# Inverses of the scan's 64x64 triangles from 8x8 blocks by products of I + powers, and decays in 65 columns a chunk

## The chip, the cores and the metric

The kernel runs on 1 core of one Trainium2 chip. The metric is the device time of one execution in microseconds (us); the time of a kernel is the median over its runs.

## The reference, cut to what matters

The program computes two blocks of a diffusion-like model and a mixture of experts. The change lies in the recurrence of the first block, which runs twice (once in each of its two layers), over a context of 256 tokens and then 512 tokens, in both directions, for 8 heads of 64 channels:

```python
def wkv_scan(r, k, v, decay, kk, a, s0, reverse, emit):
    xs = tuple(jnp.swapaxes(t, 0, 1) for t in (r, k, v, decay, kk, kk * a))

    def step(s, inp):
        r_t, k_t, v_t, w_t, kk_t, b_t = inp
        sa = -jnp.einsum("bhvk,bhk->bhv", s, kk_t)
        s = (s * w_t[:, :, None, :] + sa[..., None] * b_t[:, :, None, :]
             + v_t[..., None] * k_t[:, :, None, :])
        y = jnp.einsum("bhvk,bhk->bhv", s, r_t) if emit else None
        return s, y
...
        decay = jnp.exp(-DECAY_SCALE * jax.nn.sigmoid(decay_b0[d] + jnp.tanh(w_lo) @ decay_up[d]))
        a = jax.nn.sigmoid(iclr_b0[d] + a_lo @ iclr_up[d])
```

In chunks of 64 tokens the recurrence becomes matrix products. Inside a chunk the terms `sa` depend on one another through a strictly triangular 64x64 matrix N, so each chunk, head and direction needs the inverse (I - N)^-1.

## The kernel before, in words

All engines execute their own instruction stream in order; the tile framework orders the streams from the program's generators at build time. TensorE is PE here, VectorE DVE, ScalarE ACT, GpSimd POOL, SyncE SP.

**Steps of a scan.** `scan` runs 12 steps per layer: 4 pairs of heads, and for each pair 3 groups of 256 tokens (4 chunks). A step handles both directions and the two heads of the pair, which lie in partitions 0 to 63 and 64 to 127 and so in opposite quadrants of PE. `chunks` (L979 on) is the recurrence itself. For every chunk and direction it makes the right-hand side psR on PE (L986, L989), negates it on DVE (L992), multiplies by the inverse XI on PE (psS, L996), copies the result on ACT (L998), makes the new state psM on PE (L1004), scales the old state on POOL (L1008), adds the two on DVE (L1009), and makes the outputs pyo on PE (L1016, L1019).

**Work laid between.** `among` walks through the chunks and lets two other streams advance beside them: `others` (convolution, modulation weights, outputs of finished pairs) and `to_come`, which prepares the later steps. In step s it runs `inverse_of(s + 1)`, `blocks_of(s + 2)` and `decays(s + 3)`.

- `decay` (L849 to L876): two products pz on PE, tanh on ACT, a running sum over 64 columns a chunk on DVE (L863) with one subtraction forward (L866) or two operations backward (L870, L871), and three exponentials on ACT: P and Pp (decay up to and before a token) and Pi.
- `products` (L887 to L913): six multiplications of 128x256 on DVE, then the products pg on PE (L906), masked on DVE into GM (L910, L913). N is one half of a GM tile.
- `solve` (L680 to L694): writes N to DRAM (`nsc`, 2 DMAs for each direction, on SP), the backward direction after a 32x32 transpose on DVE (L680), reads back the 64 diagonal blocks of 16x16 as one tile NB of 64 partitions, inverts the blocks by 14 pairs of small DVE operations (L689, L690) and writes them to `xsc` in DRAM.
- `solved` (L702): loads the block inverses of a step with 4 DMAs. `transposed` copies transposes of keys and values by PE and ACT (pt L925, L926; pv L932, L933).
- `inverse` (L948 to L967): merges 16 to 32 and 32 to 64. For each level and direction: a transpose on DVE (L948), 8 products N X on PE (py, L954), a copy on ACT (L957), 8 products with XI on PE (pw, L963), and a predicated copy on DVE into the off-diagonal part (L967).

Before step 0 the streams run one after the other: `decays(0)`, `blocks_of(0)`, `decays(1)`, `inverse_of(0)`, `blocks_of(1)`, `decays(2)`.

In the trace one fp32 matmul leaves two MATMUL records; 16 products of 64x64 are 32 records. `scanbuf`, `XT` and `RK` are large buffers in which the scan's small tiles lie, so that rows name them and not N, X or XI.

Of the kernel before, what the change touches and what calls it, by code (L numbers as in the profile page):

```python
# [28 lines left out]
CH = 64  # L29
# [19 lines left out]
OTHERS = [14] * 12  # L49


def shape_constants():
# [16 lines left out]
    cf["scan"] = np.broadcast_to((np.arange(256) % CH != 0).astype(np.float32), (128, 256))  # L69
    ci = []  # L70
    for d in range(2):
        for m in (16, 32):
            pm, fm = p % 64 // m, f[:, 0:64] // m
            if d == 1:
                pm, fm = fm, pm
            ci.append(((pm // 2 == fm // 2) & (pm % 2 == 0) & (fm % 2 == 1)).astype(np.float32))
# [6 lines left out]
    return cat(cols[0]), names, cat(ci + cols[1])  # L83


NMASK = 4 * 64
# [42 lines left out]
def tile_two_blocks(ctx: ExitStack, tc: tile.TileContext, I: dict, out: bass.AP, dump=None, stop=None):  # L129
# [39 lines left out]
    CM = wk.tile([128, NMASK], I8, name="CM")  # L169
    CB = wk.tile([128, nm - NMASK], BF16, name="CB")  # L170
    cmf = wk.tile([128, nm], F32, name="cmf", tag="big", bufs=4)
    nc.gpsimd.dma_start(cmf, I["const_m"])
    nc.gpsimd.tensor_copy(CM, cmf[:, 0:NMASK])
    nc.gpsimd.tensor_copy(CB, cmf[:, NMASK:nm])
# [463 lines left out]
    def scan_buffers(first_time, RK):  # L638
# [4 lines left out]
        for name, n, cnt in (("GM", 1024, 6), ("KR", 512, 6), ("Z", 512, 4), ("BT", 512, 4), ("XI", 256, 4), ("BK", 512, 4), ("XY", 512, 2),  # L643
                             ("Mn", 128, 4)):
            ring[name] = []
            for _ in range(cnt):
                sp = next(q for q in spans if q[1] + n <= q[0].shape[1])
                ring[name].append(sp[0][:, sp[1]:sp[1] + n])
                sp[1] += n
        if first_time:  # L650
            z = SB[0][:, 0:64 * BP // 128]
# [16 lines left out]
    BP = 128 * 16 + 16  # L668
    NSC, XSC = ([dr.tile([1, 64 * BP], F32, name=f"{n}{i}") for i in range(2)] for n in ("nsc", "xsc"))
    blocks = lambda t: t[0].rearrange("(b x) -> b x", x=BP)[:, 0:2048].rearrange("b (i t) -> b i t", t=128)[:, :, 0:16]  # L670
# [3 lines left out]
    def solve(s, T, gs):  # L674

# [7 lines left out]
        NB = wk.tile([64, 16, 16], F32, name="NB", tag="nb", bufs=1)  # L683
        nc.sync.dma_start(NB, blocks(NSC[s % 2]))
        yield
        for k in range(1, 15):
            t = wk.tile([64, 64], F32, name="nbt", tag="nbt", bufs=1)[:, 0:k * (15 - k)].rearrange("p (a b) -> p a b", a=k)
            sh = [64, k, 15 - k]
            nc.vector.tensor_tensor(t, NB[:, 0:k, k:k + 1].to_broadcast(sh), NB[:, k:k + 1, k + 1:16].to_broadcast(sh), op=OP.mult)  # L689
            nc.vector.tensor_tensor(NB[:, 0:k, k + 1:16], NB[:, 0:k, k + 1:16], t, op=OP.add)  # L690
            if k % 2:
                yield
        nc.vector.tensor_scalar(NB.rearrange("p a b -> p (a b)")[:, 0:256:17], ones[0:64, 0:16], 1.0, None, op0=OP.mult)
# [3 lines left out]
    def solved(s, T, gs, get):  # L697
        for q, (d, _) in zip(T, gs):
            XI, XY = get("XI").rearrange("p (c t) -> p c t", c=4), get("XY").rearrange("p (a c t) -> p a c t", a=2, c=4)
            q.update(XI=XI, X=XY[:, 0], Y=XY[:, 1])  # L700
            for h in range(2):
                nc.sync.dma_start((q["X"] if d else q["XI"])[HR[h]], own(XSC[s % 2], d, h))  # L702

    def scan(l, S):
# [43 lines left out]
        def inverse_of(s):  # L748
            solved(s, Ts[s], parts(s)[2], get)
            yield from every(transposed, s)  # L750
            yield from inverse(Ts[s], parts(s)[2])
# [90 lines left out]
    def decay(q, l, S, pr, d, g):  # L842
# [9 lines left out]
        tA = wk.tile([128, 4, 256], F32, name="tA", tag="spl", bufs=4)  # L852
        tB = wk.tile([128, 4, 256], F32, name="tB", tag="spl", bufs=4)
        c4 = lambda v: v.rearrange("p (c t) -> p c t", t=CH)
        sa = tA[:, 0:2]
        for i in range(2):
            nc.scalar.activation(tA[:, i], pz[i][:, 0:256], AF.Tanh, scale=0.5,
                                 bias=HB[:, 8 * i + 4 * d + pr:8 * i + 4 * d + pr + 1])
        nc.scalar.activation(sa, sa, AF.Copy, scale=0.5, bias=0.5)
        yield  # L860
        sg, a = tA[:, 0], tA[:, 1]
        cum, oth = tA[:, 2], tA[:, 3]
        nc.vector.tensor_tensor_scan(cum, cst("scan"), sg, 0.0, op0=OP.mult, op1=OP.add)  # L863
        P, Pi, Pp, tmp = tB[:, 0], tB[:, 1], tB[:, 2], tB[:, 3]
        if d == 0:
            nc.vector.tensor_tensor(oth, cum, sg, op=OP.subtract)  # L866
            incl, excl = cum, oth
# [9 lines left out]
        q.update(ts=ts, a=a, P=P, Pi=Pi, Pp=Pp, tmp=tmp)  # L877
        yield

    def products(q, l, S, pr, d, g, KK, get, emit):  # L880

        RK = S["RK"]
        ts, a, P, Pi, Pp, tmp = (q[n] for n in ("ts", "a", "P", "Pi", "Pp", "tmp"))
# [3 lines left out]
        nc.vector.tensor_tensor(KR[:, 0], KK[:, ts], Pp, op=OP.mult)  # L887
        nc.vector.tensor_tensor(tmp, KK[:, ts], a, op=OP.mult)
        nc.vector.tensor_tensor(BK[:, :, 1], c4(tmp), c4(Pi), op=OP.mult)
        nc.scalar.activation(a, a, AF.Identity, scale=vc("k_a", 4 * l + pr), bias=KC[:, pr, 0:1])  # L890
        nc.vector.tensor_tensor(a, a, RK[:, 1, pr % 2, ts], op=OP.mult)
        nc.vector.tensor_tensor(BK[:, :, 0], c4(a), c4(Pi), op=OP.mult)
        if emit:
            nc.vector.tensor_tensor(KR[:, 1], RK[:, 0, pr % 2, ts], P, op=OP.mult)

        PC = wk.tile([128, 4], F32, name="PC", tag="pc", bufs=6)
        nc.vector.tensor_copy(PC, c4(P)[:, :, 63 if d == 0 else 0])
# [39 lines left out]
    def inverse(T, gs):  # L937

        bc = lambda v: v[:, None, :].to_broadcast([128, 4, 64])
        ch4 = lambda v: v[:, 0:256].rearrange("p (c t) -> p c t", c=4)  # L940

        def each(f):
            for q, (d, _) in zip(T, gs):
                f(q, d)

        def first(q, d):
            a = ("X", "XI") if d == 0 or i else ("XI", "X")
            nc.vector.transpose(q[a[0]], q[a[1]])  # L948

        def left(q, d):  # L950
            q["p"] = ch4(bank("iv", None, "py"))
            for c in range(4):
                for h in range(2):
                    nc.tensor.matmul(q["p"][HR[h], c], lhsT=q["NT"][HR[h], c], rhs=q["X"][HR[h], c], start=True, stop=True)  # L954

        def out_(q, d):
            nc.scalar.activation(q["Y"], q["p"], AF.Copy)  # L957

        def right(q, d):
            q["p"] = ch4(bank("iv", None, "pw"))  # L960
            for c in range(4):
                for h in range(2):
                    nc.tensor.matmul(q["p"][HR[h], c], lhsT=q["Y"][HR[h], c], rhs=q["XI"][HR[h], c], start=True, stop=True)  # L963

        def merge(q, d):
            mk = CM[:, (2 * d + i) * 64:(2 * d + i + 1) * 64]
            nc.vector.copy_predicated(q["XI"], bc(mk), q["p"])  # L967

        for i in range(2):
            for f in (first, left, out_, right, merge):  # L970
                each(f)
                yield
# [1209 lines left out]
```

## Time and profile before

| | |
|---|---|
| median of 3 runs | 4025.75 us (4024.86 to 4033.54) |
| the profiled execution | 4035.13 us, its span 4033.3 us |
| busy over the span | PE 3787.4 (94%), PEld 2847.6 (71%), DVE 2757.5 (68%), ACT 1707.5 (42%), POOL 330.9 (8%) |
| window taken for the first scan, from its first psS | 347 to 690 us |
| window taken for the second scan | 1581 to 1891 us |

Busy is the union of an engine's records in time. A matmul record of 64 columns lasts 0.22 us, but the next one starts long before it ends, so that PE is shown busy through the tail of each short burst. What PE could still take has to be read from how closely records follow each other. PEld is the loading of weights, which overlaps the matmuls. A row of the groups view gives the count, the busy time, the mean length of one, and the idle time of the engine just before with what ended it. The four sections of the page that this document uses are the busy times, the groups, the windows and the timeline.

### The profile page before, as it was taken

The page shows a single profiled execution, that of the slowest core. Times are in us where ns is not written, and L with a number is a line of the kernel's source. Part 1 is how long each engine was busy: PE and PEld are TensorE (multiplying, and loading weights), DVE is VectorE, ACT ScalarE, POOL GpSimd, SP SyncE. Part 2 cuts the span into 40 slices and gives each one's busy share as a digit, 9 for nine tenths or more (in the row PEclk, how much of TensorE's full clock was granted, in tenths as well). Part 3 has the DMA queues.
Part 4 walks back from the last instruction along what each step waited for, and adds up shares of the span by engine and source line. Part 5 has one row for each costly group of instructions (what it writes and reads, how often), then busy time and mean ns, then how long its engine had stood idle before and what let it go on. Part 6 is the DMA issues. An engine that isn't in the chain of part 4 may idle for free. (4 is left out here: it accounts for less than half of the span.)

```text
span 4033.3 us, 69782 instructions
## 1 busy us (share of the span) xinstructions
PE 3787.4 (94%) x27963; PEld 2847.6 (71%) x27963; DVE 2757.5 (68%) x5535; ACT 1707.5 (42%) x2552; POOL 330.9 (8%) x301
## 2 busy tenths in 40 slices
PE   6998999999999998899999998997999999999997
PEld 4786777788888786776787786675565777764443
DVE  4778875753433778876745455657877899987776
ACT  3234352321212334442322244544655676666565
POOL 0000111000000000110000000001101122122111
PEclk8999999999999998899999998997999999999999
DMA  6122323332422221123545421035979899998996
GB/s 206 44 79 67 113 65 95 124 126 84 126 79 90 96 71 27 32 42 107 164 138 165 108 81 42 1 117 186 348 289 347 304 360 369 369 353 327 373 370 241
DMA packets 353980, 677.87 MB, mean 168 GB/s; under 512 B 118760, under 2 KB 230195, under 8 KB 323539
## 3 DMA queue, kind: packets, MB, share of 16 engines
q1 hardware_dynamic: 343024, 636.89, 45.1%
q0 software_dynamic: 9376, 34.63, 3.4%
q8 instruction: 221, 3.62, 0.4%
q10 hardware_dynamic: 1250, 1.85, 0.1%
q14 instruction: 109, 0.89, 0.1%
HBM read 635.39 MB, written 37.90 MB: 167 GB/s over the span
## 5 line engine op out<-in xcount | busy, mean ns | idle before, releaser
L431 ACT ACTIVATE wh<-wst 128x1024 fp32r<-128x1024 f32 (+2 forms) x222 | 222.8, 1004 | 988.9 <-PE pc L441 519.9
L1795 DVE TENSOR_TENSOR ml<-E,mh 128x2048 fp32r<-128x2048 f32 x236 | 536.1, 2286 | 92.0 <-PE pu L1843 44.3
L1794 ACT ACTIVATE mh<-E 128x2048 fp32r<-128x2048 f32 x236 | 447.7, 1916 | 187.6 <-PE pu L1843 147.5
L441 PE MATMUL px<-Hh,wl 128*128 128x512 f32 (+2 forms) x1216 | 485.9, 400 | 15.6 <-DVE wl L432 15.5
L441 PE MATMUL px<-Hh,wh 128*128 128x512 f32 (+3 forms) x1216 | 485.3, 401 | 13.6 <-ACT wh L431 7.1
L441 PE MATMUL px<-Hl,wh 128*128 128x512 f32 (+3 forms) x1216 | 484.7, 399 | 1.0 <-DVE Hl L419 1.0
L432 DVE TENSOR_TENSOR wl<-wst,wh 128x1024 fp32r<-128x1024 f32 (+2 forms) x222 | 255.4, 1152 | 270.5 <-ACT wh L431 268.2
L1843 PE MATMUL pu<-ml,ch 128*64 128x512 f32 (+2 forms) x968 | 273.0, 399 | 21.1 <-DVE ml L1795 20.9
L1843 PE MATMUL pu<-mh,ch 128*128 128x512 f32 (+1 forms) x968 | 280.2, 404 | 6.9 <-DVE ch L1831 4.2
L441 PEld LDWEIGHTS px<-Hh,wl 128*128 128x128 f32 (+1 forms) x1216 | 231.0, 190 | 74.7 <-DVE wl L432 20.9
L441 PEld LDWEIGHTS px<-Hh,wh 128*128 128x128 f32 (+1 forms) x1216 | 231.4, 191 | 72.9 <-ACT wh L431 9.7
L441 PEld LDWEIGHTS px<-Hl,wh 128*128 128x128 f32 (+1 forms) x1216 | 231.2, 190 | 57.0 <-DVE Hl L419 5.0
L533 DVE SCALAR_TENSOR_TENSOR acc<-ZC,VT,acc 128x272 f32<-128x272 f32 (+2 forms) x600 | 253.6, 479 | 2.6 <-ACT acc L528 2.5
L1843 PEld LDWEIGHTS pu<-mh,ch 128*128 128x128 f32 (+1 forms) x968 | 172.4, 185 | 86.8 <-issue 25.4
L1795 DVE TENSOR_TENSOR ml<-st,mh 128x2048 fp32r<-128x2048 f32 x86 | 196.0, 2286 | 42.8 <-PE pu L1843 24.5
L1843 PEld LDWEIGHTS pu<-ml,ch 128*64 128x64 f32 (+2 forms) x968 | 149.8, 159 | 90.7 <-DVE ml L1795 32.3
L441 PE MATMUL pc<-Hh,wh 128*128 128x256 f32 x672 | 192.9, 288 | 0.9 <-ACT Hh L418 0.9
L441 PE MATMUL pc<-Hl,wh 128*128 128x256 f32 x672 | 191.7, 285 | 0.5 <-DVE Hl L419 0.5
L441 PE MATMUL pc<-Hh,wl 128*128 128x256 f32 (+1 forms) x672 | 190.4, 284 | 0.1
L1794 ACT ACTIVATE mh<-st 128x2048 fp32r<-128x2048 f32 x86 | 163.2, 1917 | 55.4 <-PE pu L1843 31.7
L315 DVE SCALAR_TENSOR_TENSOR as<-adt,CS,as 128x512 f32<-128x512 f32 x224 | 161.3, 747 | 33.8 <-DMA adt<-in_w_ada_dram 19.4
L1099 DVE SCALAR_TENSOR_TENSOR XT<-px,MOD,XT 128x512 f32<-128x512 f32 x66 | 49.5, 750 | 188.9 <-PE px L441 188.6
(596 smaller groups left out, 7949.8 us busy)
## 6 DMA issues: line engine op xcount, KB each, us to landing
E<-in_w_mlp_dram SPq DMA_DIRECT2D x288, 1024.0 KB
st<-in_w_mlp_dram SPq DMA_DIRECT2D x94, 1024.0 KB
wst<-in_w_in_dram SPq DMA_DIRECT2D x29, 1024.0 KB
adt<-in_ada_w_dram SPq DMA_DIRECT2D x96, 256.0 KB
adt<-in_w_ada_dram SPq DMA_DIRECT2D x96, 256.0 KB
wst<-in_ffn_wg_dram SPq DMA_DIRECT2D x22, 1024.0 KB
wst<-in_ffn_wu_dram SPq DMA_DIRECT2D x22, 1024.0 KB
adaw<-in_ada_w_dram SPq DMA_DIRECT2D x16, 1024.0 KB
```

The costliest lines, as they stand in the source:

```text
L315: nc.vector.scalar_tensor_tensor(acc[s], t, c, acc[s], op0=OP.mult, op1=OP.add)
L431: nc.scalar.activation(wh, t[:, :, c0:c0 + n], AF.Copy)
L432: nc.vector.tensor_tensor(wl, t[:, :, c0:c0 + n], f32(wh), op=OP.subtract)
L441: nc.tensor.matmul(p[0:m, 0:n], lhsT=wa[:, k, 0:m], rhs=ha[:, k, a:a + n], start=k == 0 and first, stop=k == nk - 1 and last)
L533: nc.vector.scalar_tensor_tensor(o, z[:, j + a:j + a + n], cw(j), o, op0=OP.mult, op1=OP.add)
L1099: nc.vector.scalar_tensor_tensor(o, src, gate, o, op0=OP.mult, op1=OP.add)
L1794: nc.scalar.activation(wh, t, AF.Copy)
L1795: nc.vector.tensor_tensor(wl, t, f32(wh), op=OP.subtract)
L1843: nc.tensor.matmul(p[0:xa.shape[2]], lhsT=xa[:, kt], rhs=w[part][:, c:c + 512], start=kt == 0 and j == 0, stop=last and j == len(parts) - 1)
```

## The change

The constant masks for the merges are gone; a mask `scoff` (1 outside the 8x8 diagonal blocks) comes in.

- **`solve`**: blocks of 8x8 instead of 16x16, so NB has 128 partitions and 6 pairs of DVE operations of 6 to 12 columns. After the DMAs to `nsc` are issued, POOL multiplies N by `scoff` in place (once for each direction, 128x256), which leaves N without its diagonal blocks.
- **`inverse`**: both directions go through one PSUM bank. With X the block inverses, R = X N' (N' the masked N) is a matrix whose eighth power is zero, and the inverse is X (I + R)(I + R^2)(I + R^4) in the order that the transposes ask for. PE makes 9 products of 16 matmuls of 64x64: one transposes X, two make R and its transpose, three square, three multiply on I + power. The `+ I` is a pair of matmuls of the identity with 512 columns (L945) that opens the accumulation. After each product ACT copies 128x512 out of PSUM (L955). The DVE transposes and predicated copies of `inverse` are gone.
- **`decay`**: each chunk has 65 columns, the first one zero (a POOL memset, L855), so that one running sum and one exponential hold both "up to" and "before"; forward needs no subtraction, backward one, and there are two exponentials.
- **`products`**: one 128x512 multiplication makes both halves of BK.

```diff
-        NB = wk.tile([64, 16, 16], F32, name="NB", tag="nb", bufs=1)
+        NB = wk.tile([NBLK, BLK, BLK], F32, name="NB", tag="nb", bufs=1)
         nc.sync.dma_start(NB, blocks(NSC[s % 2]))
+        for q in T:
+            nc.gpsimd.tensor_tensor(q["NT"], q["NT"], cst("scoff")[:, None].to_broadcast([128, 4, 64]), op=OP.mult)
         yield
-        for k in range(1, 15):
...
+        n = BLK - 1
+        for k in range(1, n):
...
     def solved(s, T, gs, get):
+        XX = get("XX").rearrange("p (e c t) -> p e c t", e=4, c=4)
         for q, (d, _) in zip(T, gs):
...
             for h in range(2):
-                nc.sync.dma_start((q["X"] if d else q["XI"])[HR[h]], own(XSC[s % 2], d, h))
+                nc.sync.dma_start(XX[HR[h], 1 if d else 2], own(XSC[s % 2], d, h))
...
+        nc.gpsimd.memset(full[:, 0, :, 0:1], 0.0)
...
+        nc.vector.tensor_tensor_scan(tA[:, 520:780], cst("scan"), tA[:, 0:260], 0.0, op0=OP.mult, op1=OP.add)
+        if d:
+            rest = c4(tB[:, 516:776])
+            nc.vector.tensor_tensor(rest, sums[:, :, 64:65].to_broadcast([128, 4, 65]), sums, op=OP.subtract)
+            sums = rest
...
-        nc.scalar.activation(P, incl, AF.Exp, scale=-CDEC)
-        nc.scalar.activation(Pi, incl, AF.Exp, scale=CDEC)
-        nc.scalar.activation(Pp, excl, AF.Exp, scale=-CDEC)
+        nc.scalar.activation(E, sums, AF.Exp, scale=-CDEC)
+        nc.scalar.activation(Pi, sums[:, :, incl], AF.Exp, scale=CDEC)
...
-    def inverse(T, gs):
+    def inverse(T, XX, get):
...
+        def product(a, b, plus=None):
+
+            p = bank("iv", None, "pi").rearrange("p (d c t) -> p d c t", d=2, c=4)
+            if plus is not None:
+                for h in range(2):
+                    nc.tensor.matmul(p[HR[h]].rearrange("p d c t -> p (d c t)"), lhsT=ident[HR[h], HR[h]],
+                                     rhs=plus[HR[h]].rearrange("p d c t -> p (d c t)"), start=True, stop=False)
+            for d in range(2):
+                for c in range(4):
+                    for h in range(2):
+                        nc.tensor.matmul(p[HR[h], d, c], lhsT=a[d][HR[h], c], rhs=b[d][HR[h], c] if b else ident[HR[h], HR[h]],
+                                         start=plus is None, stop=plus is None or d == 1 and c == 3)
+            return p
+
+        def to(o, p):
+            nc.scalar.activation(fl(o), fl(p), AF.Copy)
+
+        p = product([XX[:, 2], XX[:, 1]], None)
+        yield
+        to(XX[:, 0:4:3], p)
+        yield
+        p = product(N, two(X))
+        yield
+        to(R, p)
+        p = product(two(X), N)
+        yield
+        to(RT, p)
+        p = product(two(R), two(XR_), XR_)
+        yield
+        to(XR_, p)
+        n = 2 * BLK
+        while n < 64:
+
+            last = 2 * n == 64
+            p = product(two(RT), two(R))
+            yield
+            p2 = None if last else product(two(R), two(RT))
+            to(X, p)
+            yield
+            if not last:
+                to(RT, p2)
+            p = product(two(X), two(XR_), XR_)
+            yield
+            to(XT_ if last else XR_, p)
+            yield
+            X, R = R, X
+            n *= 2
```

Outside the two scans the order of every engine's stream is as before. Inside them the framework lays the streams anew. On PE, in step 6 of the first scan, before the change, from one psS to the psM after it (L1071, L1072 and L1066 belong to a finished pair, L954 and L963 to the inverse of the step to come):

```order
L996 MATMUL psS<-rg,XT 64x64 x4
L1071 MATMUL gate<-GL,GUP 128x512
L954 MATMUL py<-XT,scanbuf_2187 64x64 x16
L963 MATMUL pw<-XT 64x64 x16
L1072 MATMUL gate<-GL,GUP 128x512
L954 MATMUL py<-XT,scanbuf_2187 64x64 x16
L1066 MATMUL bon<-zz_2194,CF 128x256
L1004 MATMUL psM<-scanbuf_2188 64x64 x8
```

and in the same step after it (L899 is pg, L950 a product of the inverse, L945 the identity with 512 columns, L1012 psS, L1020 psM, L1060 and L348 a finished pair):

```order
L899 MATMUL pg<-scanbuf_2186,XT 64x128 x32
L950 MATMUL pi<-XT,scanbuf_2185 64x64 x16
L1060 MATMUL gvar<-CF,zz_2192 128x2 x6
L1012 MATMUL psS<-rg,XT 64x64 x4
L950 MATMUL pi<-scanbuf_2185,XT 64x64 x16
L945 MATMUL pi<-XT,CF 64x512
L1020 MATMUL psM<-scanbuf_2186 64x64 x8
L945 MATMUL pi<-XT,CF 64x512
L950 MATMUL pi<-XT 64x64 x16
L348 MATMUL spread<-CF,zz_2192 128x128 x6
```

The products of the inverse now stand in nearly every link of the chunk's chain, with the identity pairs among them.

On POOL, in the first scan, the stream before the change (L1008 is the old state times its decay, L803 a reload of keys):

```order
L1008 TENSOR_SCALAR XT<-XT,PC 128x64 x28
L803 DMA RK<-rkd_2184 128x768 x2
L1008 TENSOR_SCALAR XT<-XT,PC 128x64 x16
L803 DMA RK<-rkd_2184 128x768 x2
L1008 TENSOR_SCALAR XT<-XT,PC 128x64 x16
```

and after it, over about one step (L1024 is the old state times its decay, L678 the masking of N, L855 the zero columns):

```order
L798 DMA RK<-rkd_2182 128x768 x2
L1024 TENSOR_SCALAR RK<-RK,PC 128x64 x6
L855 MEMSET tA 128x4 x2
L1024 TENSOR_SCALAR RK<-RK,PC 128x64 x2
L678 TENSOR_TENSOR scanbuf_2185<-scanbuf_2185,CB 128x4x64 x2
L1024 TENSOR_SCALAR RK<-RK,PC 128x64 x4
L855 MEMSET tA 128x4 x2
```

The two maskings and two memsets of each step stand between the state's multiplications, which had POOL almost to themselves.

## Rows read from the trace of the kernel before

**Rows 1.** Windows view; busy us (count) of PE, PEld, DVE, ACT, POOL, then PEclk, DMA share, GB/s.
```profile
347.00:690.00 343.00, 320.84 (x6198) 254.15 (x6195) 263.99 (x971) 137.36 (x349) 42.88 (x84) 0.99 0.32 87
1581.00:1891.00 310.00, 285.28 (x5845) 233.27 (x5840) 236.16 (x899) 131.94 (x349) 47.05 (x84) 0.95 0.21 47
```

**Rows 2.** Timeline of PE in the first scan (start us, us, what, xrecords).
```profile
561.10 1.10 PE L963 MATMUL pw<-XT 64*64 64x64 f32 x32
...
582.28 3.84 PE L906 MATMUL pg<-scanbuf,XT 64*64 64x128 f32 x64 [2.11 <-DVE XT L892]
```

**Rows 3.** Groups by form, PE, 347 to 690 us; xrecords | busy us, mean ns | idle before.
```profile
L1019 PE MATMUL pyo<-scanbuf,scanbuf 64*64 64x64 f32 x716 | 46.0, 219 | 1.6 <-DVE VY L1030 1.0 <-ACT scanbuf L998 0.6
L906 PE MATMUL pg<-scanbuf,XT 64*64 64x128 f32 x576 | 40.0, 278 | 7.3 <-DVE XT L892 5.4 <-issue 1.9
L954 PE MATMUL py<-XT,scanbuf 64*64 64x64 f32 x704 | 31.4, 225 | 4.6 <-DVE XT L948 2.6 <-DMA XT<-xsc 1.8
...
L849 PE MATMUL pz<-WA,DUP 64*128 64x256 f32 x64 | 19.5, 428 | 0.2 <-ACT tA L857 0.2
L782 PE MATMUL pco<-ZC,wst 128*128 128x512 f32 x38 | 17.9, 609 | 0.0
...
L932 PE MATMUL pv<-CF,VY 64*64 64x64 f32 x320 | 11.9, 220 | 0.2 <-issue 0.2
...
L542 PE MATMUL cmean<-acc,CF 128*128 128x256 f32 x4 | 1.4, 432 | 0.0
```

**Rows 4.** Groups by form, PE, 1581 to 1891 us.
```profile
L1019 PE MATMUL pyo<-scanbuf,scanbuf 64*64 64x64 f32 x499 | 34.7, 219 | 0.3 <-ACT scanbuf L998 0.3
...
L906 PE MATMUL pg<-scanbuf,XT 64*64 64x128 f32 x384 | 28.9, 285 | 2.0 <-DVE scanbuf L910 1.1 <-DVE XT L892 0.9
...
L849 PE MATMUL pz<-WA,DUP 64*128 64x256 f32 x70 | 23.2, 444 | 0.5 <-ACT tA L857 0.5
L782 PE MATMUL pco<-ZC,wst 128*128 128x512 f32 x44 | 21.0, 611 | 0.0
...
L906 PE MATMUL pg<-scanbuf,XT 64*64 64x64 f32 x192 | 8.5, 252 | 4.0 <-DVE XT L892 3.9
...
L548 PE MATMUL cvar<-CF,acc 128*128 128x2 f32 x16 | 2.1, 254 | 0.0
```

**Rows 5.** Lines L948, L967 and L689, whole program; ns min/median/max.
```profile
L948 DVE STREAM_TRANSPOSE XT<-XT x96: 392/436/447, 336.8 to 1866.6; 128x256 f32<-128x256 f32 x96
L967 DVE COPY_PREDICATED XT<-CM,pw x96: 400/440/450, 339.8 to 1870.6; 128x256 f32<-128x256 int8 x96
L689 DVE TENSOR_TENSOR nbt<-NB x336: 135/189/245, 314.7 to 1856.2; 64x14 f32<-64x14 f32 x24, 64x36 f32<-64x36 f32 x24, 64x50 f32<-64x50 f32 x24, 64x56 f32<-64x56 f32 x24
```

**Rows 6.** Groups by form, DVE and ACT, 347 to 690 us.
```profile
L910 DVE TENSOR_TENSOR scanbuf<-pg,CB 128x512 f32<-128x512 f32 x36 | 24.5, 682 | 4.5 <-PE pg L906 4.2
...
L889 DVE TENSOR_TENSOR XT<-tB 128x256 f32<-128x256 f32 x18 | 7.4, 412 | 0.1
...
L897 DVE COPY PC<-tB 128x4 f32<-128x4 f32 x18 | 2.8, 158 | 0.0
...
L926 ACT ACTIVATE XT<-pt 128x512 f32<-128x512 f32 x11 | 6.4, 592 | 9.2 <-PE pt L925 8.9 <-PE psM L1004 0.3
```

**Rows 7.** Timelines of SP and POOL around one issue of the blocks.
```profile
585.00 1.38 SPq L682 DMA_DIRECT2D nsc<-scanbuf  x2
587.42 1.23 SPq L682 DMA_DIRECT2D nsc<-Nt  x2
590.28 0.59 SPq L684 DMA_DIRECT2D NB<-nsc  x1
588.84 0.86 POOL L1008 TENSOR_SCALAR XT<-XT,PC 128x64 f32<-128x64 f32 x2 [4.01 <-DVE XT L1009]
```

**Rows 8.** Timeline of DVE before the first chunk: one blocks loop, its ends.
```profile
314.72 0.17 DVE L689 TENSOR_TENSOR nbt<-NB 64x14 f32<-64x14 f32 x1 [0.42 <-DMA NB<-nsc]
330.67 0.17 DVE L690 TENSOR_TENSOR NB<-NB,nbt 64x14 f32<-64x14 f32 x1
```

More of the change, by code (lines that the diff above doesn't have):

```diff
@@ L49 @@
 OTHERS = [14] * 12
+BLK = 8
 def shape_constants():
@@ L68, in shape_constants @@
     cf["sel4"] = (p % 32 == np.arange(4)[None, :]).astype(np.float32)
[L69 to L76, printed above, removed]
+    cf["scan"] = np.broadcast_to((np.arange(4 * CH + 4) % (CH + 1) != 0).astype(np.float32), (128, 4 * CH + 4))
+    cf["scoff"] = (p % 64 // BLK != f[:, 0:64] // BLK).astype(np.float32)
     names, cols = {}, ([], [])
@@ L642, in scan_buffers @@
         ring = {}
-        for name, n, cnt in (("GM", 1024, 6), ("KR", 512, 6), ("Z", 512, 4), ("BT", 512, 4), ("XI", 256, 4), ("BK", 512, 4), ("XY", 512, 2),
+        for name, n, cnt in (("GM", 1024, 6), ("KR", 512, 6), ("Z", 512, 4), ("BT", 512, 4), ("XI", 512, 2), ("BK", 512, 4), ("XX", 1024, 1), ("RR", 1024, 1),
                              ("Mn", 128, 4)):
@@ L665, in tile_two_blocks @@
     CS_ = [slice(CH * c, CH * c + CH) for c in range(4)]
-    BP = 128 * 16 + 16
-    NSC, XSC = ([dr.tile([1, 64 * BP], F32, name=f"{n}{i}") for i in range(2)] for n in ("nsc", "xsc"))
-    blocks = lambda t: t[0].rearrange("(b x) -> b x", x=BP)[:, 0:2048].rearrange("b (i t) -> b i t", t=128)[:, :, 0:16]
+    NBLK = 8 * 128 // BLK
+    BP = 128 * BLK + BLK
+    NSC, XSC = ([dr.tile([1, NBLK * BP], F32, name=f"{n}{i}") for i in range(2)] for n in ("nsc", "xsc"))
+    blocks = lambda t: t[0].rearrange("(b x) -> b x", x=BP)[:, 0:128 * BLK].rearrange("b (i t) -> b i t", t=128)[:, :, 0:BLK]
     whole = lambda t, q: t[0].rearrange("(q c x) -> q c x", q=2, c=4)[q, :, 0:16384].rearrange("c (p t) -> p c t", t=128)
@@ L748, in inverse_of @@
         def inverse_of(s):
-            solved(s, Ts[s], parts(s)[2], get)
+            XX = solved(s, Ts[s], parts(s)[2], get)
             yield from every(transposed, s)
-            yield from inverse(Ts[s], parts(s)[2])
+            yield from inverse(Ts[s], XX, get)
         def blocks_then_decays(s):
@@ L851, in decay @@
         yield
[L852 to L855, printed above, removed]
+        tA = wk.tile([128, 1024], F32, name="tA", tag="spl", bufs=4)
+        tB = wk.tile([128, 1024], F32, name="tB", tag="spl", bufs=4)
+        c4 = lambda v: v.rearrange("p (c t) -> p c t", c=4)
+        full, sums = tA[:, 0:520].rearrange("p (i c t) -> p i c t", i=2, c=4), c4(tA[:, 520:780])
@@ L882, in products @@
         RK = S["RK"]
-        ts, a, P, Pi, Pp, tmp = (q[n] for n in ("ts", "a", "P", "Pi", "Pp", "tmp"))
+        ts, sa, P, Pi, Pp = (q[n] for n in ("ts", "sa", "P", "Pi", "Pp"))
         c4 = lambda v: v.rearrange("p (c t) -> p c t", t=CH)
@@ L935, in transposed @@
         yield
-    def inverse(T, gs):
[L939 to L952, printed above, removed]
-                for h in range(2):
[L954 to L972, printed above, removed]
@@ new lines, in inverse @@
+    def inverse(T, XX, get):
+        RR = get("RR").rearrange("p (e c t) -> p e c t", e=4, c=4)
+        XT_ = get("XI").rearrange("p (d c t) -> p d c t", d=2, c=4)
+        fl = lambda v: v.rearrange("p d c t -> p d (c t)")
+        X, XR_, R, RT = XX[:, 0:2], XX[:, 2:4], RR[:, 0:2], RR[:, 2:4]
+        N = [q["NT"] for q in T]
+        two = lambda v: [v[:, 0], v[:, 1]]
+        def product(a, b, plus=None):
+            p = bank("iv", None, "pi").rearrange("p (d c t) -> p d c t", d=2, c=4)
+            if plus is not None:
+                for h in range(2):
+                    nc.tensor.matmul(p[HR[h]].rearrange("p d c t -> p (d c t)"), lhsT=ident[HR[h], HR[h]],
[34 more added lines that the diff above has]
+            to(XT_ if last else XR_, p)
+            yield
+            X, R = R, X
+            n *= 2
+        for q, XI in zip(T, two(XT_)):
+            q["XI"] = XI
```

63 lines of the change are left out of this document (24 added, 39 removed).

## The prediction

> **What bounds the kernel now.** The change touches only the two scans, so I first read the windows view over them [rows 1]. DVE is busy 264.0 of 343 us and 236.2 of 310 us, PE 320.8 and 285.3. Neither engine is full, and PE's figure says too much, because it counts the 0.22 us tail of every small matmul. So I rebuild PE's work from the rate at which records follow each other. In the timeline 32 records of 64x64 take 1.10 us from the first start to the last end; less the length of the last one, 0.22 us, that is 0.88 us over 31 steps, 28.4 ns a record. 64 records with 128 columns take 3.84 us; less 0.28 us, over 63 steps, 56.5 ns a record [rows 2].
>
> First window [rows 3]: the eleven groups of 64x64 (the first, L1019, with 716 records, the last, L932, with 320) hold 5120 records, 145.4 us. L906 holds 576 x 56.5 ns = 32.5 us. L849 is taken at its busy time, 19.5 us. The 17 other groups (17.9 us for the first, 1.4 us for the last) have 93.4 us of busy time, which is too much rather than too little. Sum 291 us; in the remaining 52 us PE waits. Second window [rows 4]: twelve groups of 64x64 from 499 down to 192 records hold 5233, 148.6 us; L906 in its 128-column form 21.7, L849 23.2, and nine other groups (21.0 to 2.1 us) 50.3. Sum 244 us, 66 us of waits. So PE is the fuller engine (85% and 79%), DVE comes next (77% and 76%), and the two wait for each other: before L906 and L954, for instance, PE stands still for DVE, 5.4 and 2.6 us in the first window [rows 3].
>
> **The change part by part.**
>
> *PE, inverse.* A product of 16 matmuls is 32 records, 32 x 28.4 ns = 0.91 us. An inverse for both directions was 64 matmuls, 3.64 us. It becomes 9 products, 8.18 us, and three identity pairs. A pair is 4 records of 512 columns; the trace has none in quadrants. Scaled from the 128-column record (4 x 56.5 ns) a record is 0.226 us and a pair 0.90 us. The upper bound is that the two halves do not overlap, twice this, 1.81 us. The lower bound is that the pair costs no more than one of 128 columns, 0.23 us. I take 0.90, since the 128-column rows are quadrant pairs as well and the cost has there doubled with the columns, from 28.4 to 56.5 ns. So an inverse is 8.18 + 2.71 = 10.89 us, 7.25 us more. Each window holds 11 of the 12 inverses (the first runs ahead of it): +80 us in each. By the bounds on the pair it would be 58 to 110 us.
>
> *DVE.* Off go 96 transposes of 436 ns (41.9 us) and 96 predicated copies of 440 ns (42.2 us) [rows 5]. The blocks' loop had 336 pairs of 189 ns operations (L689 [rows 5]; its partner L690 is as long), 127 us; 144 pairs remain, of 6 to 12 columns, for which the nearest row is the 4-column copy L897, 158 ns [rows 6]: 45.5 us, so 81.5 off. The running sum loses 48 operations of 412 ns, 19.8 us (L889's form). In the products two multiplications of 412 ns become one of 682 ns (L910's form) 48 times, 6.8 us off [rows 6]. Sum 192 us, 8 us a step. DVE then has about 176 of 264 and 148 of 236 us, and no longer paces a step.
>
> *ACT.* 216 copies of 128x512 out of PSUM at 592 ns (L926 [rows 6]) add at most 128 us, against 96 smaller copies and 48 exponentials taken away. ACT was busy 137 and 132 us [rows 1], so it has room. A copy that stands ahead of the chunk's own copy can delay it by 0.6 us. That is hidden while PE has a product to run, and costs up to that much where it has none.
>
> *SP and DRAM.* The same number of DMAs. The blocks are as many pieces (128 x 8 instead of 64 x 16 rows), half as long. The load comes half a step after the store, so a longer landing stays hidden.
>
> *POOL.* Two maskings and two memsets a step, ahead of the state's multiplications (a rival, below). I take nothing for them.
>
> *Ahead of the first chunk.* The blocks' loop runs from 314.7 to 330.8 us there [rows 8]; 6 of 14 rounds remain, at most 9 us less. The inverse that follows is 7 us longer on PE and has more copies in its chain, at most 10 us more. I take 0, with 9 us either way for each scan.
>
> **The sum.** With no wait left at all PE needs 291 + 80 = 371 us in the first window and 244 + 80 = 324 in the second, 28 and 14 us more than they last now: +42 us. Of today's 118 us of waits those for DVE should mostly go. Those inside the chain of a chunk remain where no product fills them (PE to DVE and back, PE to ACT and back). Bounds: none remain, or all. I take a third, 39 us, because the order shows products in nearly every link. Together +81 us. Against the profiled execution, 4035.1 us, that is 4116; it stands 9.4 us above the median of the runs, and on the median, 4025.75, I forecast 4107 us. About 0.2%, 8 us, is what a measurement of this kernel tells from no change.
>
> The granted clock was 0.95 in the second window and 0.99 in the first [rows 1]. A PE with fewer gaps may hold it; 0.05 x 310 us is 15.5 us of lost work at most, which belongs to the low end.
>
> **Rivals.**
>
> *DVE was the pace and PE takes the products for less (faster).* The place is PE's burst of products. The price of one must fall from 0.91 us to p for the change to break even: 535 us of work in both windows, 22 x (12p - 3.64) us of new work and 39 us of waits reach the 653 us of now at p = 0.60. For it: DVE loses 192 us, and PE waits for it before L906 and L954 [rows 3]. Against it: 32 records of the very same kind take 1.10 us [rows 2]. At p = 0.50 the scans lose 27 us, 3999 us. Here a rule of the Trainium skill speaks against my sum: the page Perfetto Trace Analysis, section Identifying the Most-Contended Engine, says that matmul busy time is a poor measure for TensorE, that one should take the busy share of the weight loads, and that the engine with the highest occupancy is the one to relieve. By it DVE (264.0 and 236.2 us) stands ahead of the weight loads (254.2 and 233.3 us) [rows 1], and a change that relieves DVE wins. In rows of this case: the loads' 487 us spread over 12,043 records are 40 ns each, 22 inverses add 172 records each, so the loads would fill 640 of 653 us; if they were the only limit the time would be 4013 us. I give that 0.03 of the faster case's 0.09. The trace agrees with the rule about busy time, and for that reason I rebuilt the rate; a rate of 28.4 ns a record is a harder limit than the loads' share, though.
>
> *The waits swallow it (no change).* All 118 us of waits are filled, the 143.7 us of other groups are overstated by a fifth (29 us), and each start is a few us shorter: +42 - 29 - 10 = +3, 4029 us. For it: the products are laid between the links of the chain. Against it: it wants PE full from end to end in both scans, which no stretch of them shows.
>
> *POOL holds up the state (slower still).* The forward masking waits until both DMAs have read N. In the trace they are issued from 585.00 to 586.38 us. The backward ones end at 588.65, and the read-back that waits for them is issued at 590.28, so a landing takes 1.6 us [rows 7]. POOL then stands from about 585 to 588 us. Each of the two maskings takes between one state multiplication, 0.43 us, and four times that, as it has 256 columns against 64. So POOL is free at 588.9 to 591.4 us, while the state's multiplication ran at 588.84 [rows 7]: 0.1 to 2.6 us late in each of 24 steps, 2 to 62 us. At half of that, 32 us on top, 4139 us.
>
> **How the numbers follow.** My forecast, PE as the pace of both scans, 0.68 and 4107 us. POOL on top 0.15. No change 0.08. Faster 0.09. The forecast's own bounds are +42 - 29 - 18 = -5 us, were all of it lucky, and +42 + 118 = +160 us with every wait kept. The low end with half of that luck is +14, 4040 us. The high end is the forecast with two thirds of the waits kept (+121 us) and part of POOL's delay (+28), 4175 us. What lies below 4040 us is the faster and the unchanged case, 0.17, and I leave out little above. Faster 0.09, same 0.08, slower 0.83.
>
> **What would show it.** L950 should have 3456 matmuls at 28 ns a record in bursts, L945's pairs near 0.9 us. DVE should be busy some 90 us less in each scan and PE should wait less, while the scans last some 35 to 45 us longer each. The first psS of each scan should come within 9 us of where it is now, counted from the scan's first decays. If products take under 0.6 us, or L1009's counterpart waits for POOL, a rival holds. If the scans last as long as before and PE's records follow without gaps, my count of PE's work was too high.

## The result and the profile after

The changed kernel takes 4127.25 us (median of 4 runs, 4125.04 to 4133.30) against 4026.24 for the kernel before on the same chip: 1.0249 times as long, 95% interval 1.0232 to 1.0267. Forecast were 4107 us and a range of 4040 to 4175. The profiled execution took 4126.31 us, span 4124.5. The page's busy times (us, share of the span, records), the whole program:

```profile
PE 3906.9 (95%) x32091; PEld 2954.2 (72%) x32091; DVE 2641.0 (64%) x4863; ACT 1776.7 (43%) x2625; POOL 369.9 (9%) x396
```

DVE has 116.5 us less than in the kernel before, PE 119.5 more, ACT 69.2 more. The windows view, each scan from its first psS to its last (columns as in [rows 1]):

```profile
340.00:751.50 411.50, 398.29 (x8318) 318.43 (x8316) 219.26 (x687) 173.00 (x396) 63.99 (x122) 1.00 0.28 78
1631.00:1983.50 352.50, 336.58 (x7678) 277.14 (x7676) 187.53 (x600) 164.89 (x386) 61.16 (x120) 1.00 0.18 40
```

In the kernel before, the same stretches ran from 346.7 to 701.5 and from 1583.9 to 1890.9 us, 354.8 and 307.0 us long, with PE busy 331.1 and 282.3, DVE 267.7 and 233.8, and a granted clock of 0.99 and 0.95 (compare [rows 1]). So the scans last 56.7 and 45.5 us longer; ahead of and between them 6.7 and 2.9 us are saved.

PE in the second scan, groups by form (answering to [rows 4]):

```profile
L950 PE MATMUL pi<-XT 64*64 64x64 f32 x2112 | 77.6, 220 | 0.0
L945 PE MATMUL pi<-XT,CF 64*64 64x512 f32 x132 | 37.3, 591 | 0.0
L1002 PE MATMUL psR<-scanbuf,scanbuf 64*64 64x64 f32 x376 | 28.1, 227 | 5.3 <-DVE RK L1025 5.1
L899 PE MATMUL pg<-scanbuf,XT 64*64 64x128 f32 x418 | 27.8, 272 | 3.0 <-DVE scanbuf L887 3.0
...
L844 PE MATMUL pz<-WA,DUP 64*128 64x256 f32 x72 | 16.0, 428 | 2.0 <-ACT tA L857 2.0
```

L950 and L945 are the products and the identity pairs; before either, PE stands idle for nothing in these rows. To weigh every run alike I use the prediction's rule: PE's **work** is the records in quadrants at 28.4, 56.5 and 226 ns each (64, 128 and 512 columns) plus the busy time of the rest; what is left of the scan is the **remainder**, time in which PE does not advance at its full rate. A part of it is **clock**: a stretch of T us at a mean granted clock c is taken to lose (1 - c) x T, at two decimals within some 2 us a scan. Records outside the quadrants stand in the work at their busy time, which is longer where the clock is low, so a few us are in both, by an estimate some 8 in e4 and 2 in the kernel before. Ratios are of all fast runs (one run of e10, 6949 us at a granted clock of 0.78, is left out); the other columns are of the one profiled run, which for e3 is 10 us above its median, for e8 7 and for e6 12 below. Sums over both scans, us:

| | ratio to before, 95% | scans | work | remainder | of it clock | DVE busy |
|---|---|---|---|---|---|---|
| before | 1 | 661.8 | 540.4 | 121.4 | 19 | 501.5 |
| changed | 1.0249 [1.0232, 1.0267] | 764.0 | 692.3 | 71.7 | 0 | 406.8 |
| e1 | 0.9962 [0.9948, 0.9975] | 645.4 | 537.9 | 107.5 | 12 | 486.5 |
| e2 | 1.0246 [1.0230, 1.0262] | 761.8 | 694.7 | 67.1 | 0 | 420.5 |
| e3 | 1.0160 [1.0142, 1.0179] | 733.3 | 640.4 | 92.9 | 15 | 440.8 |
| e4 | 1.0193 [1.0178, 1.0209] | 732.9 | 620.1 | 112.8 | 32 | 447.6 |
| e5 | 1.0341 [1.0302, 1.0380] | 790.4 | 712.3 | 78.1 | 4 | 406.6 |
| e6 | 1.0315 [1.0286, 1.0345] | 775.4 | 693.5 | 81.9 | 4 | 497.2 |
| e7 | 1.0409 [1.0382, 1.0437] | 808.4 | 693.7 | 114.7 | 12 | 527.7 |
| e8 | 1.0109 [1.0082, 1.0135] | 682.3 | 581.1 | 101.2 | 17 | 462.0 |
| e9 | 1.0279 [1.0249, 1.0308] | 775.6 | 693.2 | 82.4 | 4 | 546.5 |
| e10 | 1.0263 [1.0225, 1.0301] | 771.3 | 696.2 | 75.1 | 0 | 402.3 |
| e11 | 0.9937 [0.9910, 0.9963] | 636.5 | 531.0 | 105.5 | 13 | 485.8 |
| e12 | 1.0382 [1.0344, 1.0420] | 833.7 | 726.6 | 107.1 | 24 | 489.0 |

The change in this account: work +152, clock -19, other remainder -31, together the +102 us by which the scans grew. Times of runs in different sets came from chips whose kernel before stood between 4019 and 4026 us, so the text compares ratios; 0.001 is 4 us.

### The profile page after: what moved, and what is told of

The parts are those of the page before. It is cut to its first block, busy times and chain, and to the rows that moved or that the text cites. A ratio compares the mean times of both kernels' runs of the same rounds, so it can differ in the third digit from the quotient of the medians.

```text
span 4124.5 us, 77709 instructions
## 1 busy us (share of the span) xinstructions
PE 3906.9 (95%) x32091; PEld 2954.2 (72%) x32091; DVE 2641.0 (64%) x4863; ACT 1776.7 (43%) x2625; POOL 369.9 (9%) x396
## 5 line engine op out<-in xcount | busy, mean ns | idle before, releaser
L431 PE MATMUL px<-Hh,wh 128*128 128x512 f32 (+3 forms) x1216 | 485.6, 401 | 13.7 <-ACT wh L421 7.1
L955 ACT ACTIVATE XT<-pi 128x512 f32<-128x512 f32 x216 | 128.8, 596 | 317.7 <-PE pi L950 315.0
L950 PEld LDWEIGHTS pi<-XT 64*64 64x64 f32 x4608 | 161.2, 135 | 36.7 <-issue 23.7
```

Of the source, the lines that this page charges most:

```text
L431: nc.tensor.matmul(p[0:m, 0:n], lhsT=wa[:, k, 0:m], rhs=ha[:, k, a:a + n], start=k == 0 and first, stop=k == nk - 1 and last)
L950: nc.tensor.matmul(p[HR[h], d, c], lhsT=a[d][HR[h], c], rhs=b[d][HR[h], c] if b else ident[HR[h], HR[h]], start=plus is None, stop=plus is ...
L955: nc.scalar.activation(fl(o), fl(p), AF.Copy)
```

## Experiments

The theory on trial, A: TensorE's work sets the scans' length in the changed kernel. The rivals stand in each expectation, with their numbers and letters; what they come to is that the chain from product to copy to product paces, so that TensorE's work is hidden, or that VectorE's load does, so that its relief paid for much of the products.

### The two halves of the change, e1 and e2

e1 is the kernel before with `decay` and `products` of the change (and the mask `scan`); e2 is the change with those of the kernel before. One line of the edit of e1, which e2 has the other way round:

```diff
-        nc.vector.tensor_tensor_scan(cum, cst("scan"), sg, 0.0, op0=OP.mult, op1=OP.add)
+        nc.vector.tensor_tensor_scan(tA[:, 520:780], cst("scan"), tA[:, 0:260], 0.0, op0=OP.mult, op1=OP.add)
```

> The kernel before with the new decays and products (65 columns a chunk) and the old inverse. Theory A, PE paces the scans: DVE does 27 us less and ACT 20 us less, PE the same, so 0 to 10 us faster, 4016 to 4026 us. Theory B, DVE paced the scans before: most of the 27 us come off the time, 4000 to 4010 us.

> The changed kernel with the old decays and products, so only the new blocks and inverse are in. Theory A: the whole loss is the inverse's, 4122 to 4137 us. Theory B: without the 27 us of DVE relief the loss is larger, 4145 to 4155 us.

e1 took 4006.79 us, 0.38% less than the kernel before, within the 4000 to 4010 of its expectation's B and under the 4016 to 4026 of A; e2, 4119.62 us or 1.0246, cannot be told from the whole change. So the slowdown is the inverse's, and the decays are worth 15 us beside the old inverse and nothing beside the new one. In e1 the scans are 16.4 us shorter with DVE 15.0 and ACT 18.4 us less busy and PE's work 2.5 us less; 7 us of the gain are clock by the table. So some of the waits beside the old inverse went with the load of DVE and ACT; which of the two it was, no run separates. In the changed kernel the same relief (13.7 us of DVE, table) brings nothing.

### Taking TensorE work away, e3, e4 and e8

e3 drops the identity pairs and adds on DVE instead of copying on ACT, three times an inverse; e4 starts from blocks of 16, which saves three products and a pair; e8 does both.

```diff
-                    nc.tensor.matmul(p[HR[h]].rearrange("p d c t -> p (d c t)"), lhsT=ident[HR[h], HR[h]],
-                                     rhs=plus[HR[h]].rearrange("p d c t -> p (d c t)"), start=True, stop=False)
...
+        def plus(o, p):
+            nc.vector.tensor_tensor(fl(o), fl(p), fl(XR_), op=OP.add)
```

```diff
-BLK = 8
+BLK = 16
```

> The changed kernel without the identity pairs: the three sums I + power are made by DVE as it copies the product out of PSUM, in place of the copy on ACT. 72 pairs of 0.9 us, 65 us of PE, go; 72 additions of 0.68 us, 49 us of DVE, come. Theory A: 50 to 65 us faster than the changed kernel, 4062 to 4077 us. Theory C, the waits between product and copy pace the inverse and PE's own work is hidden: at most 20 us faster, 4107 us or more.

> The changed kernel with blocks of 16x16: three products and one identity pair fewer in an inverse (3.6 us of PE, 87 us in all) and the old loop of 14 pairs on DVE (82 us more). Theory A: 65 to 87 us faster than the changed kernel, 4040 to 4062 us. Theory B, DVE's relief is what counts: no faster than the changed kernel, 4127 us or more.

> The changed kernel with blocks of 16 and with the additions on VectorE, both edits that took TensorE work out of it, together: 24 x (3.6 + 1.8) us, 130 us of 261 that the inverses have. If each returns what it did alone (a quarter to a half of the work, 22 and 36 us), 4062 to 4085. If something else has become the pace (VectorE's load, the links of the chain), no better than the better of the two, 4085 to 4100. If TensorE's work alone counts, 4000 to 4030.

Against the change, e3 won 0.0089 (36 us), e4 0.0056 (23 us) and e8 0.0140 (56 us). e3 lies between the 50 to 65 us of A and the 20 at most of C, e4 between the 65 to 87 of A and the nothing of B, and e8, 4061.10 us, at the edge of the range for edits that return what they did alone (36 + 23 = 59). The windows view says where the rest went; e4, both scans, then two stretches of the second:

```profile
343.40:732.40 389.00, 372.81 (x7169) 290.74 (x7165) 240.15 (x837) 152.31 (x352) 57.70 (x120) 0.97 0.31 83
1615.10:1959.00 343.90, 316.52 (x6527) 256.49 (x6524) 207.48 (x751) 142.62 (x340) 59.61 (x118) 0.94 0.18 43
1835.00:1855.00 20.00, 17.58 (x286) 13.63 (x283) 9.50 (x47) 9.11 (x21) 2.82 (x6) 0.74 0.10 16
1875.00:1895.00 20.00, 15.87 (x185) 10.90 (x182) 13.51 (x53) 7.29 (x18) 0.00 (x0) 0.74 0.17 45
```

The granted clock is 0.97 and 0.94, and 0.74 in two stretches of 20 us, where TensorE was at 1.2 GHz for about half of the time; in the changed kernel it was 1.00 in both scans. PE's timeline in those two stretches of e4:

```profile
1842.48 0.48 PE L1012 MATMUL psS<-rg,XT 64*64 64x64 f32 x4 [2.42 <-DVE rg L1008]
...
1878.83 0.33 PE L1002 MATMUL psR<-scanbuf,scanbuf 64*64 64x64 f32 x4 [3.60 <-DVE RK L1025]
...
1886.43 3.57 PE L918 MATMUL pt<-CF,XT 64*64 64x64 f32 x64
```

In each PE had just stood still for DVE, 2.42 and 3.60 us. The low clock is a real loss: 64 records take 3.57 us, where 64 x 28.4 ns are 1.8. e4 has 72 us less work and scans 31 us shorter: 32 us went to the clock and 9 to other waits. In e3 it is 52 us of work, 31 won, 15 clock and 6 other; in e8 111, 82, 17 and 12. (The 82 us of e8 became 56 in the ratio: its first scan starts 7 us later than the change's, its profiled run is 7 us under its median, and on its chip the kernel before took 6 us less.) So theory A holds with an addition: work taken from TensorE does come back, less what a lower clock and other waits take.

e8, both scans:

```profile
347.40:721.40 374.00, 355.27 (x7076) 285.12 (x7073) 247.43 (x859) 138.53 (x328) 64.34 (x120) 0.97 0.32 87
1606.10:1914.40 308.30, 288.61 (x6441) 239.19 (x6437) 214.60 (x772) 129.18 (x317) 58.23 (x118) 0.98 0.21 48
```

### Adding load, e5, e6, e9 and e7

e5 puts one more product into each inverse; e6 and e9 put two additions on DVE behind each copy, in e6 of constants, in e9 of what the copy wrote; e7 is the kernel before with eight products in each inverse (`more` is one product of 16 matmuls). The diffs of e5, e9 and e7 (of e7 the place where the products are called):

```diff
         to(RT, p)
+        product(two(X), N)
         p = product(two(R), two(XR_), XR_)
```

```diff
             nc.scalar.activation(fl(o), fl(p), AF.Copy)
+            for _ in range(2):
+                t = wk.tile([128, 256], F32, name="dum", tag="dum", bufs=1)
+                nc.vector.tensor_tensor(t, fl(o)[:, 0], fl(o)[:, 1], op=OP.add)
```

```diff
                 each(f)
+                if f is not first:
+                    more()
                 yield
```

> The changed kernel with one more product of 16 matmuls in each inverse, its result unused: 24 x 0.91 us, 21.8 us of TensorE work, and nothing for any other engine. Theory A (TensorE sets the pace of the scans, because 72 us of waits are all that is left in 764 us of both): 14 to 22 us above the changed kernel's 4127, 4141 to 4149. Theory B (the chain from product to copy to product sets the pace and TensorE has room in its waits): at most 7 us more, up to 4134.

> The changed kernel with two additions of 128x256 on VectorE, their results unused, behind each of the nine copies of an inverse: 216 x 2 x 0.41 us, 177 us, so that VectorE has about the load of the kernel before again (569 of 764 us in the two scans), while TensorE has the changed kernel's. Theory A (TensorE paces the changed kernel; VectorE's relief was not what the time went by): 0 to 30 us above 4127. Theory C (the relief of VectorE has paid for a good part of the new products): half of the 177 us or more comes back, 4215 and above.

> The kernel before, all as it was, with eight products of 16 matmuls added to each inverse, their results unused: 24 x 8 x 0.91 us, 175 us, as much as the change adds to TensorE, without its relief of VectorE, its copies or its chain. Theory A (TensorE's work alone makes the change slow): 80 to 105 us above the kernel before, about where the changed kernel stands, 4105 to 4130. Theory C (with VectorE's old load the waits would stay): 130 us or more above it, 4155 and up. Theory B (the changed kernel is slow by its chain of copies and not by TensorE's work): under 60 us above it, below 4085.

> The run before of this kind missed its aim: most of its additions ran long before their place, since they read only constants. Here the two additions of 128x256 behind each of the nine copies of an inverse read what the copy has just written, so they stand in their place in both scans: 198 x 2 x 0.41 us, 162 us of VectorE work in the two windows, its load near 569 of 764 us. Theory A (TensorE paces the changed kernel, VectorE's relief returns nothing there): 0 to 30 us above the changed kernel's 4127 (ratio to the kernel before 1.025 to 1.032). Theory C (the relief has paid for a good part of the products; the kernel before with the products added is 62 us above the changed kernel): 50 us or more above it, ratio 1.037 and up.

e5: 0.0092 above the change, 37 us by the ratios (whose intervals are 16 and 7 us to either side) and 25 by the profiled spans. The scans grew by 26 us, 20 of them the work of 22 products, none of it hidden. By the ratios that is above the 14 to 22 us of A, by the spans near it; B, with 7 us at most, is out.

e6 failed as a test: 177 of its additions ran before the first scan and 255 in it, none in the second. Its first scan, the only loaded one, grew by 15 us for 91 us more of DVE. It stood 0.0066 above the change all the same; the profiled run, 4130 us, is the shortest of its four, so its trace cannot show where the other runs' time went. e9 has them in their place:

```profile
344.10:765.90 421.80, 403.34 (x8322) 322.11 (x8319) 290.32 (x885) 173.50 (x396) 71.12 (x122) 0.99 0.28 76
1645.50:1999.30 353.80, 336.77 (x7674) 276.89 (x7669) 256.15 (x798) 164.31 (x385) 66.73 (x120) 1.00 0.18 40
```

DVE has 140 us more in the scans than in the change, 45 more than in the kernel before, and the scans grow by 12 us (0.0030 of the time, 12 us too, with intervals that overlap). VectorE's load is not what the changed kernel goes by, and its relief is worth little there. C falls.

e7 has the changed kernel's work within 2 us, and was 162 us above the kernel before where A had said 80 to 105:

```profile
350.40:782.20 431.80, 404.96 (x9202) 339.69 (x9198) 279.34 (x967) 141.02 (x359) 48.03 (x86) 0.99 0.27 74
1665.80:2042.40 376.60, 348.12 (x8576) 300.77 (x8573) 248.36 (x882) 131.99 (x349) 45.03 (x84) 0.98 0.17 39
```

Its number is C's, but the reason behind C fell with e9. Read by the account it is simpler: 153 us of work were added and the remainder went from 121 to 115. In the old order of the inverse the gaps are hardly filled by added products, in the new one 31 us of them are, beside the clock. The scans of e7 are 44 us longer than the change's at the same work: PE is shown idle for 55 us of them against 29, and 12 are clock. A part of the idle time is of the test's own making; among PE's longest waits in e7, first scan, then second:

```profile
PE pada L294 <- DVE XT L967: 5.9, 2, 3.9
...
PE pm L974 <- DVE XT L967: 5.4, 6, 1.2
```

L967 is the merge on DVE, which empties a PSUM bank; L974 is an added product, and L294 a product for the modulation weights. Both take their bank from the ring that the inverse uses.

### Where the filled gaps came from, e12, e10 and e11

e12 is e7 without the DVE transposes and merges of the old inverse, so the larger blocks stay unfilled:

```diff
         def first(q, d):
-            a = ("X", "XI") if d == 0 or i else ("XI", "X")
-            nc.vector.transpose(q[a[0]], q[a[1]])
+            pass
...
-            nc.vector.copy_predicated(q["XI"], bc(mk), q["p"])
+            pass
```

> The kernel before with the eight added products of the seventh run, and without the transposes and the predicated copies of its inverse: 192 VectorE operations, 84 us, are left out (the inverse of the 16x16 blocks is used as it is loaded, no larger blocks are filled in). TensorE's work is that of the seventh run (4182, 1.0409 of the kernel before). What is open is why that run was some 60 us slower than the changed kernel at the same TensorE work. If the turns to VectorE inside the inverse hold TensorE's queue up: 40 to 85 us less than that run, ratio 1.020 to 1.031, where the changed kernel stands. If they do not: within 15 us of it, ratio 1.037 to 1.045.

At 1.0382 it is 11 us under e7, inside the bound for "they do not". The table is less clear than that: the remainder without the clock fell from 103 to 83 us, while the clock took 12 us more, and the scans began earlier, so that part of the first inverse lies within them. The turns to VectorE held some of the time: PE's idle time in the scans fell from 55 to 41 us, and no wait for the merge is left. They do not make the whole difference between e7 and the change, 0.0160 of the time or 64 us; where the rest comes from is left open.

e10 and e11 spread the pieces laid between the chunks' links over all of them, in the change and in e1:

```diff
-AHEAD = 16
+AHEAD = 22
```

> The changed kernel with the pieces that are laid between the chunks' links spread over all of them: AHEAD 22 for 16, so that at most one or two of the 20 or 21 pieces of a step are left over at its end instead of 4 or 5. If the 72 us of waits stand where links have no product beside them: 20 to 40 us less than 4127, ratio 1.015 to 1.020. If TensorE's work is all and the waits lie elsewhere: within 10 us of it, ratio 1.0225 to 1.0275. If the inverse then comes too late for the next step's chunks: slower, 4140 and above.

> The kernel before with the new decays alone (0.9962 of the kernel before) and AHEAD 22 for 16, the same edit as in the changed kernel. If the 108 us of waits stand where links have no product beside them: 20 to 50 us less, ratio 0.984 to 0.991. If they belong to the round trips between TensorE and VectorE, whatever lies between: within 10 us, ratio 0.9935 to 0.9985. If the blocks or the inverse come too late: slower, ratio above 0.9985.

e10 stayed within the noise of the change (1.0263), and its remainder at 75 us: the leftover pieces at the end of a step are not where the waits lie. e11 took 3996.98 us, 0.9937 of the kernel before, the shortest time of the study; its interval overlaps e1's, so the gain over e1 (10 us) is likely and not proven. Its remainder, 105.5 against 107.5 us, did not move, so the spread is not shown to fill waits there either. Both scans:

```profile
343.70:684.90 341.20, 327.51 (x6374) 261.11 (x6369) 259.36 (x937) 127.90 (x328) 49.98 (x102) 0.98 0.34 93
1563.40:1858.70 295.30, 273.49 (x5735) 221.85 (x5731) 226.41 (x848) 120.65 (x317) 44.65 (x100) 0.98 0.22 49
```

## Why the prediction was right, and where its steps were off

**The case was the forecast's: PE paces both scans.** The time was 20 us above 4107. About 10 of these are the base: the sum was made against a profiled run 9.4 us above its median, and the profiled run of the changed kernel is not above its own. The span grew by 91.2 us where 81 were forecast. That PE paces rests on e5, where 20 us of added work cost 26, and on e9, where 140 us of DVE cost 12. That the sum came within 10 us is in part luck: its terms missed by 29, 8 and 10 us, the first one up and the others down (below).

**PE's work: right.** Forecast +80 us in each scan, measured +78.1 and +73.8. L950 has 6912 records, the 3456 matmuls named. The timeline of PE in the first scan:

```profile
570.61 0.69 PE L950 MATMUL pi<-scanbuf,XT 64*64 64x64 f32 x18
571.13 0.59 PE L945 MATMUL pi<-XT,CF 64*64 64x512 f32 x1
571.14 0.32 PE L1020 MATMUL psM<-scanbuf 64*64 64x64 f32 x2
571.57 0.59 PE L945 MATMUL pi<-XT,CF 64*64 64x512 f32 x1
571.99 0.56 PE L1020 MATMUL psM<-scanbuf 64*64 64x64 f32 x13
572.40 0.59 PE L945 MATMUL pi<-XT,CF 64*64 64x512 f32 x1
572.40 0.22 PE L1020 MATMUL psM<-scanbuf 64*64 64x64 f32 x1
572.46 0.39 PE L950 MATMUL pi<-XT 64*64 64x64 f32 x4
572.83 0.59 PE L945 MATMUL pi<-XT,CF 64*64 64x512 f32 x1
573.26 0.92 PE L950 MATMUL pi<-XT 64*64 64x64 f32 x25
...
582.43 1.08 PE L945 MATMUL pi<-XT,CF 64*64 64x512 f32 x4
583.34 1.10 PE L950 MATMUL pi<-XT 64*64 64x64 f32 x32
584.27 0.63 PE L1020 MATMUL psM<-scanbuf 64*64 64x64 f32 x16
```

A pair takes 0.91 us here (582.43 to 583.34; 0.90 was taken), 0.86 in the median of the 43 pairs with no other record between; a product takes 0.93 (583.34 to 584.27; 0.91). The scaling of the pair from 128 columns, the step with the widest bounds, was right.

**The waits kept: the term that was mis-sized.** The prediction wrote: "I take a third, 39 us, because the order shows products in nearly every link." Of 121 us (118 in the prediction's slightly shorter windows) 71.7 were kept, more than half: 50 us went instead of 79, +29 on the sum. The work, 8 under the forecast, and the starts, 10 under it, took back 18. And what went was in part of another kind: 19 us were not waits for an engine but a clock below full speed, which came back (0.99 and 0.95 [rows 1], now 1.00 at two decimals). The prediction had named that and put it at the low end only. Of the waits proper, about 102 us, 72 stayed. The windows view parts them: PE is shown idle for 13.2 and 15.9 us of the scans (411.50 less 398.29, 352.50 less 336.58), 29 us where it was 48 before, and the other 43 us lie in time in which it is shown busy. The stops are many and short; in the first scan after, the longest entries of PE in the waits view are

```profile
PE psR L1002 <- DVE RK L1025: 2.4, 2, 1.6
PE pz L844 <- ACT tA L857: 2.2, 8, 0.4
```

(us in all, times, longest), in the second 5.1 us in 6 stops for the first of these. The 43 us fit short bursts, whose last record's 0.22 us no later one covers; that is argued and not shown.

**VectorE: half of the forecast.** Said were 192 us less over the program and "some 90 us less in each scan"; it was 116.5, and 48 and 46 in the scans. The counts were right (672 records fewer), the price was not: a record is longer than its turn. DVE's timeline ahead of the first scan, after:

```profile
308.02 0.41 DVE L882 TENSOR_TENSOR tA<-zz,tA 128x256 f32<-128x256 f32 x1
308.35 0.41 DVE L881 TENSOR_TENSOR scanbuf<-zz,tB 128x256 f32<-128x256 f32 x1
308.69 0.41 DVE L883 TENSOR_TENSOR tA<-tA,RK 128x256 f32<-128x256 f32 x1
309.02 0.41 DVE L887 TENSOR_TENSOR scanbuf<-RK,tB 128x256 f32<-128x256 f32 x1
```

Each lasts 0.41 us and starts 0.34 after the one before: 0.07 us of each is under its neighbour. The prediction had seen this of PE and not of DVE. Over the whole program the lengths of DVE's records add up to 3097 us before and 2920 after, 177 less and near the 192; but they covered each other for 340 us before and 279 after, and these 61 us are most of the 75 missing. By e9 and e2 it cost the forecast little, since VectorE's load hardly counts once PE paces.

**ACT** 69 us more (128 at most was said). **The starts** came 10 us earlier in all (within 9 us each was said).

**POOL holds up the state: did not happen.** Line L678, the masking, with what POOL's idle time before it ended with, and L1025, the counterpart of L1009, with what DVE's idle time before it ended with:

```profile
L678 POOL TENSOR_TENSOR scanbuf<-scanbuf,CB x48: 674/678/1202, 302.6 to 1924.9; 128x256 f32<-128x256 f32 x48
...
  DMA nsc<-scanbuf: 10.9, 9
...
L1025 DVE SCALAR_TENSOR_TENSOR RK<-psM,PC,RK x160: 241/283/285, 349.1 to 1982.2; 128x64 f32<-128x64 f32 x160
...
  PE psM L1020: 78.2, 44
```

The masking takes 0.68 us, inside the bounds of 0.43 and 1.72. POOL does wait for the DMAs before it, 10.9 us in 9 cases, but the view lists no engine that waited for L678, and L1025 waits for PE and never for POOL, so none of the 2 to 62 us shows.

**Faster: did not happen.** A product takes 0.93 us, not under 0.60, and VectorE's relief was not what counted. By the Trainium skill's rule (Perfetto Trace Analysis, Identifying the Most-Contended Engine), which judges TensorE's headroom by the busy share of the weight loads, VectorE came first in the kernel before and was the one to relieve. In this case: beside the old inverse that fits e1, which won 15 us with 15 us of DVE (and 18 of ACT) less in the scans; for the change as a whole the measurement decides against it. The weight loads were busy 77% of the first scan after, and yet one more product in each inverse (e5) lengthened the scans by more than its work. **No change** needed the waits to be swallowed whole; 72 of 121 us stayed. **The low end** was mis-added: half of the luck of 29 and 18 us, taken from +42, is +18, 4044 us, where +14 and 4040 stand; nothing hangs on it.

## What to carry to other kernels

Price work moved to TensorE by the rate at which its records follow each other, and expect most of it in the time of a stretch that its work nearly fills: here it filled 540 of 662 us, and 152 us more of it became 102 us of time; of the rest 19 us were a clock that came back as the gaps went, and 31 us gaps that were filled. Where gaps open again, look at the granted clock before looking for a new wait. Split a change of two halves before judging it: the decays alone, with the pieces spread wider, were 0.63% faster than the kernel before, and in company of the new inverse they showed nothing.

## What was not expected of the hardware

- An identity pair that other matmuls break up loses its overlap. In the timeline above the four records of 571.13 to 573.26 us share 2.13 us with 20 small records (0.57 us at 28.4 ns), so the pair takes 1.56 us instead of 0.91. Five of the 72 pairs had 20 or more other records among them, 24 had one to six.
- The granted clock went with TensorE's gaps and not with the amount of its work. It was 1.00 in both scans of the change; e4, with a tenth less work, lost 32 us to it, but so did e12 24 us, with more work than the change (727 against 692) and 107 us of remainder against 72. In e4 it fell right after stops of 2.42 and 3.60 us. The four runs of e3 alone, one and the same kernel, range from 4100.5 us at a granted clock of 0.963 over the whole run to 4078.6 at 0.970.
